# A two-layer hybrid trunk on one core: SSD groups with GLA heads between, and the decay logits on four row tiles

## The chip, the core and the metric

The kernel runs on one core of a Trainium2 chip. The metric is device time in microseconds. The kernel before takes 2295.11 us, the median of 3 runs (2294.96 to 2295.38).

## The reference, cut to what matters

Two layers (DEPTH = 2), a sequence of 512, D_MODEL = 1024, float32. Each layer projects the normed input to many parts at once and runs three branches on them:

```python
proj = u @ w_in
(gq, gk, gv, ga, gg, mqk, mv, mi, mf, mo, sz, sxbc, sdt, gates) = jnp.split(proj, SPLIT_POINTS, axis=-1)

log_a = jax.nn.log_sigmoid((ga @ gla_wa + gla_ba).astype(f32)) / GLA_TAU     # ga: 16 columns, gla_wa: 16 x 512
o_gla = gla(heads(gq, 4), heads(gk, 4), heads(gv, 4), heads(log_a, 4))
y_gla = group_rmsnorm(o_gla, gla_norm, GLA_HEADS) * silu(gg)
...                                                                          # mLSTM on mqk, mv, mi, mf, mo
xbc = silu(causal_dwconv(sxbc, ssd_conv_w, ssd_conv_b))
sx, sb, sc = split(xbc)                                                      # 16 heads of 64 in 2 groups
y = ssd(heads(sx, 16), softplus(sdt + bias), -exp(a_log), heads(sb, 2), heads(sc, 2))
y_s = group_rmsnorm((y + ssd_d * xh) * silu(sz), ssd_norm, SSD_GROUPS)

z = einsum('btkw,kwd->btkd', stack([y_gla, y_m, y_s]), w_branch)
h = h + sum(sigmoid(gates + gate_b) * z) @ w_out
h = h + conv_ffn(rmsnorm(h, norm_ffn), ...)                                  # width-3 conv, gated
```

Two things concern the change: the decay logits `ga @ gla_wa`, a product over 16 columns alone, and the SSD branch, whose two groups don't depend on each other.

## The kernel before, in words

Activations lie transposed: 128 channels on the partitions, 512 tokens along the free axis. Each large product is made exact to float32 by two fp32r parts of each operand, a rounded one (made by ScalarE, `act`) and the rest (made by VectorE, `tt`): three matmuls, high-high, high-low and low-high, take the place of one (`prods`). A projection of 128 output columns over 1024 input channels is 8 x 3 = 24 matmuls of 128 x 128 weights and 512 tokens. This is called a unit here. `units` makes two units from one pair of weight tiles; `units_tok` makes gv and mv with tokens on the partitions, at the same number of matmuls for 128 columns.

Weights stream from memory in the order of the list `MIX`: `load` issues a load on the SP queue into one of three raw buffers, and `prep` (priority 300) splits it into a high and a low part, in one of two buffers each. `S` is the first tile of a layer, the "small projections": columns 0 to 15 are ga, 32 to 47 sdt, 64 to 67 mi, 96 to 99 mf, the others zero. In the first layer `start` loads and splits the first two tiles in halves, between the tiles of the first norm.

The Python text gives the program order. The framework then plans each engine's instructions by its own cost estimates, in program order unless something is given priority (evictions of accumulators have 300, like `prep`), and writes out one fixed order for each engine; on the chip each engine takes its instructions in that order and waits where it must. Chains that don't belong to the units run in the background: `Bg` holds generators, and `after_unit` ticks all of them once after each unit. `bg.drain` ticks until a condition holds, without units in between. PSUM has four banks for accumulators of units and four (`mps`) for the small work.

The order in a layer (`layer`): S and twelve sxbc units with their convolutions (four taps on VectorE), while `rows` and both `ssd_group` generators run in the background; then for each two GLA heads, four units of gq and gk and four of gv; then `bg.drain` until all eight SSD outputs `sy` are there; then the four `gla_head` generators start (`stagger`, a lag of two ticks), beside eight units of sz (gate of the SSD branch), which complete the SSD branch's norm (`fin_s`); then the SSD branch's gates and output projection (`branch(u, 2, ...)`), mLSTM, gg, and so on to the MLP.

`rows` takes the output of S, called `sm`, and makes all per-token rows from it. Its first step after the biases (L524 to L529) is the decay logits: for each of four heads one float32 matmul of `wa` (128 x 128, of which 16 rows are not zero) with `sm`, and two reads of the result by ScalarE. `wa` is loaded by one DMA at the start of the layer (L877). `ssd_group` (L778) makes one group's scores (B times C), transposes its four x tiles and weights them, forms the states of the chunks, and then, for each pair of heads, the mixes (L830: a row broadcast by DMA, scalings, an exponential, a product) and two sets of small float32 matmuls: eight with 64 output columns (`bc`, `xd`) and three with 128 (`cc`, `ss`).

Of the kernel before, what the change touches and what calls it, by code (L numbers as in the profile page):

```python
# [9 lines left out]
F32 = mybir.dt.float32  # L10
F32R = mybir.dt.float32r
I32 = mybir.dt.int32
AF = mybir.ActivationFunctionType
ALU = mybir.AluOpType
# [3 lines left out]
P = 128  # L18
L = 2
D = 1024  # L20
T = 512
# [32 lines left out]
MIX = ["S"]  # L54
for _g in range(2):
    MIX += [("sxbc", 1024 + 128 * _g), ("sxbc", 1280 + 128 * _g)]
    MIX += [("sxbc", 512 * _g + 128 * _i) for _i in range(4)]
NSSD = len(MIX)

TOK = []  # L60
for _h in range(0, 4, 2):
    MIX += [("gq", 128 * _h), ("gk", 128 * _h), ("gq", 128 * _h + 128), ("gk", 128 * _h + 128)]
    TOK.append(len(MIX))
    MIX += [("gv", 256 * _h + 128 * _i) for _i in range(4)]
# [27 lines left out]
N8 = NMIX + 2 * NFF  # L92
# [41 lines left out]
class Kern:  # L134
# [122 lines left out]
    def load(self):  # L257
# [14 lines left out]
        self.raw_q.append(raw)  # L272
        self.load_at = [c, j + 1] if j + 1 < n else [c + 1, 0]

    def start(self):

        nc = self.nc
        nc.sync.dma_start(self.pars[0], self.par_in[0])
        half = KT // 2
        raws = []  # L280
        for j in range(2):
            self.n += 1
            raws.append(self.pw.tile([P, KT * P], F32, tag="raw", name=f"raw_{self.n}", bufs=RAW_BUFS))
        self.n += 1
        wh, wl = (self.pw.tile([P, KT, 2 * P], F32R, tag=t, name=f"{t}_{self.n}", bufs=W_BUFS) for t in ("wh", "wl"))
        self.split[0] = (wh, wl)
        for i in range(KT):
            self.h[i] = self.t("h")
        for k in range(2):
            ks = slice(k * half, (k + 1) * half)  # L290
            cs = slice(k * half * P, (k + 1) * half * P)
            nc.sync.dma_start(self.h[k * half], self.xT[:, k * half, :])
            for j in range(2):
                nc.sync.dma_start(raws[j][:, cs], self.w8[j][:, cs])
            for i in range(k * half + 1, (k + 1) * half):
                nc.sync.dma_start(self.h[i], self.xT[:, i, :])
        nc.sync.dma_start(self.cst, self.cst_in)
        for k in range(2):
            ks = slice(k * half, (k + 1) * half)
            cs = slice(k * half * P, (k + 1) * half * P)  # L300
            for j in range(2):
                r = raws[j][:, cs].rearrange("p (k c) -> p k c", c=P)
                o = slice(j * P, (j + 1) * P)
                self.act(wh[:, ks, o], r)
                self.tt(wl[:, ks, o], r, wh[:, ks, o].bitcast(F32), ALU.subtract)
            for i in range(k * half, (k + 1) * half):
                self.norm_tile(i)
                self.h[i] = None
        self.load_at, self.prep_at = [1, 0], [1, 0]
        self.load()  # L310
        nc.sync.dma_start(self.pars[1], self.par_in[1])
        for _ in range(RAW_BUFS - 1):
            self.load()
# [6 lines left out]
    def prep_(self):  # L320
        c, j = self.prep_at
        if c >= len(self.chunks):
            return
        if not self.raw_q:
            self.load()
        src, idx, nk, n = self.chunks[c]
        if src == 2:
            nk, n = KT // 2, 4
        raw = self.raw_q.pop(0)
        if j == 0:  # L330
            self.n += 1
            self.split[c] = (
                self.pw.tile([P, nk, n * P], F32R, tag="wh", name=f"wh_{self.n}", bufs=W_BUFS),
                self.pw.tile([P, nk, n * P], F32R, tag="wl", name=f"wl_{self.n}", bufs=W_BUFS))
        wh, wl = self.split[c]
        if src == 2:
            n = 2
            cs = slice(2 * j * P, 2 * (j + 1) * P)
            wh, wl = (w[:, :, cs].rearrange("p k (j c) -> p j k c", j=2) for w in (wh, wl))
            r = raw.rearrange("p j (k c) -> p j k c", c=P)  # L340
        else:
            wh, wl = wh[:, :, j * P:(j + 1) * P], wl[:, :, j * P:(j + 1) * P]
            r = raw.rearrange("p (k c) -> p k c", c=P)
        self.act(wh, r)
        self.tt(wl, r, wh.bitcast(F32), ALU.subtract)
        self.load()
        self.prep_at = [c, j + 1] if j + 1 < n else [c + 1, 0]
# [158 lines left out]
    def rows(self, ps):  # L506
# [12 lines left out]
        self.n += 1  # L519
        ag, ab = [la[:, h] for h in range(4)], la[:, 4]  # L520
        self.act(ab, zs, AF.Abs)
        zg = []
        yield
        for h in range(4):  # L524
            p2 = self.mps()
            self.mm(p2, self.wa[:, h * P:(h + 1) * P], sm)
            z = self.t("zg")
            self.act(z, p2, AF.Identity, bias=self.col("ba", h))
            self.act(ag[h], p2, AF.Abs, bias=self.col("ba", h))  # L529
            zg.append(z)  # L530
            if h == 1:
                yield
# [339 lines left out]
    def layer(self, l):  # L872
        nc = self.nc
        bg = self.bg
        self.par = self.pars[l]
        self.wa = self.pc.tile([P, T], F32, name=f"wa{l}", tag="wa", bufs=1)
        self.dq.dma_start(self.wa, self.wa_in[l])  # L877
        self.hpar = self.pc.tile([P, HHI - HLO], F32, name=f"hpar{l}", tag="hpar", bufs=2)
        nc.vector.tensor_scalar(self.hpar, self.par[:, HLO:HHI], 0.5, None, op0=ALU.mult)
        self.rows_ready = False  # L880
# [10 lines left out]
        def evx(i, store, j):  # L891
            def ev(ps):
                store[j] = self.silu2(*self.conv(ps, 4, "scw", i, 12, "scb", i))
            return ev
        evs = [lambda ps: bg.add(self.rows(ps))]
        for g in range(2):
            evs += [evx(8 + g, self.sb, g), evx(10 + g, self.sc, g)]
            evs += [evx(4 * g + i, self.sx, 4 * g + i) for i in range(4)]
        bg.add(self.ssd_group(0))
        bg.add(self.ssd_group(1))  # L900
        for i in range(0, NSSD, 2):
            self.wide = i < WIDE
            self.units(u, evs[i:i + 2], boundary=(i == 0), mid=(self.norm_end, self.norm_rows_of_cols))


        for h in range(4):
            def evq(ps):
                self.gq[h] = self.t("gq")
                with self.tc.high_priority(EV_PRIO):
                    self.stt(self.gq[h], ps, 128.0 ** -0.5, self.rstd, ALU.mult, ALU.mult)  # L910

            def evk(ps):
                self.gk[h] = self.t("gk")
                self.first(self.gk[h], ps)
            self.units(u, [evq, evk])
            if h % 2:
                for i in (h - 1, h):
                    self.gv[i] = Blocks([self.v() for _ in range(2)])
                self.units_tok(u, lambda b, ps: self.evac_tok(b, ps, self.gv[h - 1:h + 1]))
        bg.drain(lambda: full(self.sy))  # L920


        rsum_g = self.t("rsg")
        bg.add(self.stagger([self.gla_head(h, rsum_g) for h in range(4)], GLA_LAG))
        sqs, ready, ys, done_s = [None, None], [], [], []

        def fin_s(g):
# [21 lines left out]
        bg.add(fin_s(0))  # L949
        bg.add(fin_s(1))  # L950
        for g in range(2):
            for i in range(2):
                def evz(ps, j):
                    s = self.t("sz")
# [293 lines left out]
GLA_LAG = 2  # L1248
# [101 lines left out]
```

## Time and profile before

| | |
|---|---|
| median of 3 runs | 2295.11 us (2294.96 to 2295.38) |
| the profiled execution's own time | 2295.16 us |
| its span, first to last instruction | 2293.3 us |
| TensorE busy | 2279.3 us, 99% |
| VectorE busy | 1434.1 us, 63% |
| ScalarE busy | 902.7 us, 39% |
| mean granted TensorE clock | 0.998 of 2.4 GHz |
| DMA | 235.73 MB, 103 GB/s on average |

Busy means that an instruction of the engine was under way. Matmuls are pipelined, so a matmul's own duration (0.39 us for 512 columns) overlaps the next one's; the step from one start to the next is its price. A float32 matmul shows as two records. The rows below give times from the start of the span. In a row of the timeline the first number is the start, the second the duration, then engine, line, operation, output and inputs by the program's names, the shape, and the count of merged instructions; in brackets stands the engine's idle time before it and what ended it. L241 is the helper of every matmul, L229 that of every ScalarE instruction, L232 and L238 those of VectorE.

### The profile page before, as it was taken

The page shows a single profiled execution, that of the slowest core. Times are in us where ns is not written, and L with a number is a line of the kernel's source. Part 1 is how long each engine was busy: PE and PEld are TensorE (multiplying, and loading weights), DVE is VectorE, ACT ScalarE, POOL GpSimd, SP SyncE. Part 2 cuts the span into 40 slices and gives each one's busy share as a digit, 9 for nine tenths or more (in the row PEclk, how much of TensorE's full clock was granted, in tenths as well). Part 3 has the DMA queues.
Part 4 walks back from the last instruction along what each step waited for, and adds up shares of the span by engine and source line. Part 5 has one row for each costly group of instructions (what it writes and reads, how often), then busy time and mean ns, then how long its engine had stood idle before and what let it go on. Part 6 is the DMA issues. An engine that isn't in the chain of part 4 may idle for free.

```text
span 2293.3 us, 27258 instructions
## 1 busy us (share of the span) xinstructions
PE 2279.3 (99%) x10832; PEld 1876.8 (82%) x10832; DVE 1434.1 (63%) x2165; ACT 902.7 (39%) x1344; POOL 2.8 (0%) x22
## 2 busy tenths in 40 slices
PE   9999999999999999999999999999999999999998
PEld 6878888888888888888888788888888888888887
DVE  6966745474464587467579767345744645873774
ACT  6534632333333344234354346233333433442432
POOL 0000000000000000000000000000000000000000
PEclk9999999999999999999999999999999999999999
DMA  5253223332232333232323522232322343232222
GB/s 181 85 156 101 74 74 104 99 120 93 87 111 97 129 100 107 82 101 97 128 85 102 162 92 74 77 107 93 129 90 90 101 132 107 93 97 94 94 91 75
DMA packets 78911, 235.73 MB, mean 103 GB/s; under 512 B 8872, under 2 KB 12264, under 8 KB 78784
## 3 DMA queue, kind: packets, MB, share of 16 engines
q1 hardware_dynamic: 78784, 233.99, 31.7%
q8 instruction: 85, 1.39, 0.3%
q14 instruction: 42, 0.34, 0.1%
HBM read 229.55 MB, written 4.41 MB: 102 GB/s over the span
## 4 chain that ended last, share of the span: by engine, by line
PE 93%; DVE 4%; ACT 2%; issue 1%; DMA 1%; SPq 0%; DVEq 0%; ACTq 0%
PE acc L241 65%; PE m L241 27%; DVE cc L238 1%; PE m L244 1%; ACT la L229 1%; DVE wl L232 1%; DVE la L610 0%; DMA h<-in_xT 0%; DVE og L232 0%; DVE cx L232 0%; DMA dn<-ry 0%; ACT zg L229 0%; ACT cc L229 0%; DVE zg L238 0%; ACT wh L229 0%
## 5 line engine op out<-in xcount | busy, mean ns | idle before, releaser
L229 ACT ACTIVATE wh<-raw 128x1024 fp32r<-128x1024 f32 (+2 forms) x372 | 385.1, 1077 | 586.1 <-PE acc L241 250.9
L241 PE MATMUL acc<-uh,wh 128*128 128x512 f32 x1552 | 609.3, 393 | 2.0 <-DVE mo L232 1.0
L241 PE MATMUL acc<-uh,wl 128*128 128x512 f32 x1552 | 605.9, 391 | 0.4 <-DVE wl L232 0.3
L241 PE MATMUL acc<-ul,wh 128*128 128x512 f32 x1552 | 605.7, 390 | 0.1
L232 DVE TENSOR_TENSOR wl<-raw,wh 128x1024 fp32r<-128x1024 f32 (+2 forms) x372 | 453.2, 1250 | 154.4 <-ACT wh L229 154.0
L241 PEld LDWEIGHTS acc<-uh,wh 128*128 128x128 f32 x1552 | 291.4, 188 | 64.2 <-issue 2.7
L241 PEld LDWEIGHTS acc<-uh,wl 128*128 128x128 f32 x1552 | 291.4, 188 | 62.7 <-DVE wl L232 1.5
L241 PEld LDWEIGHTS acc<-ul,wh 128*128 128x128 f32 x1552 | 291.4, 188 | 61.6 <-DVE ul L238 1.6
L238 DVE SCALAR_TENSOR_TENSOR cc<-cx,par,cc 128x510 f32<-128x510 f32 (+2 forms) x296 | 217.6, 748 | 41.0 <-ACT cc L229 36.9
L241 PE MATMUL acc<-yl,wh 128*128 128x512 f32 x512 | 200.0, 391 | 0.0
L241 PE MATMUL acc<-yh,wl 128*128 128x512 f32 x512 | 199.7, 390 | 0.0
L241 PE MATMUL acc<-yh,wh 128*128 128x512 f32 x512 | 199.6, 392 | 0.0
L241 PE MATMUL m<-uh,wh 128*128 128x512 f32 x384 | 149.8, 390 | 1.2 <-ACT wh L229 1.2
L241 PE MATMUL m<-uh,wl 128*128 128x512 f32 x384 | 149.9, 390 | 0.0
L241 PE MATMUL m<-ul,wh 128*128 128x512 f32 x384 | 149.4, 389 | 0.0
L229 ACT ACTIVATE cc<-cx,par 128x512 f32<-128x512 f32 x128 | 102.8, 809 | 86.6 <-DVE cx L232 86.5
L241 PE MATMUL m<-ah,wl 128*128 128x512 f32 x308 | 120.0, 390 | 0.0
L241 PE MATMUL m<-al,wh 128*128 128x512 f32 x308 | 119.8, 389 | 0.0
L241 PE MATMUL m<-ah,wh 128*128 128x512 f32 x308 | 119.5, 389 | 0.0
L241 PEld LDWEIGHTS acc<-yh,wl 128*128 128x128 f32 x512 | 96.1, 188 | 20.5 <-issue 0.4
L241 PEld LDWEIGHTS acc<-yh,wh 128*128 128x128 f32 x512 | 96.1, 188 | 19.8 <-DVE gg L232 0.4
L241 PEld LDWEIGHTS acc<-yl,wh 128*128 128x128 f32 x512 | 96.2, 188 | 19.5
(204 smaller groups left out, 2653.3 us busy)
## 6 DMA issues: line engine op xcount, KB each, us to landing
raw<-in_w SPq DMA_DIRECT2D x336, 512.0 KB, 3.6
raw<-in_w SPq DMA_DIRECT2D x32, 704.0 KB, 4.0
bc<-dr SPq DMA_DIRECT2D x48, 256.0 KB, 3.6
h<-in_xT SPq DMA_DIRECT2D x16, 256.0 KB, 6.6
eb<-dr SPq DMA_DIRECT2D x32, 128.0 KB, 4.5
bc<-dn SPq DMA_DIRECT2D x16, 256.0 KB, 3.1
kept<-h SPq DMA_DIRECT2D x8, 256.0 KB, 2.0
h<-kept SPq DMA_DIRECT2D x8, 256.0 KB, 5.6
```

The source lines that it names most:

```text
L229: return self.nc.scalar.activation(out, in_, func, bias=bias, scale=scale)
L232: return self.nc.vector.tensor_tensor(out, a, b, op=op)
L238: return self.nc.vector.scalar_tensor_tensor(out, a, s, b, op0=op0, op1=op1)
L241: return self.nc.tensor.matmul(out, lhsT, rhs, start=start, stop=stop)
L244: return self.nc.tensor.transpose(out, x, self.ident)
```

## The change

It has two parts.

The order: `MIX` now has group 0 of the SSD projections (sb, sc and four sx tiles), two GLA heads' projections, group 1 of the SSD projections, and the other two GLA heads'. `layer` follows it with `ssd_proj(g)`. The first drain asks only for the four outputs of group 0; the second asks for the others ahead of the sz units of group 1, and the `gla_head` generators are added there instead of ahead of all sz units.

The decay logits: `spread` copies the columns of ga in the raw S tile to columns 48, 80 and 112, so that `sm` has ga in rows 0 to 15, 48 to 63, 80 to 95 and 112 to 127. The weights of head h are put in the same rows of one 128 x 128 tile, by eight loads, and split into a high and a low part, as is `sm`. Each head's logits are then three fp32r matmuls on 32 rows (rows 32h to 32h+31), in three passes over the heads, to four PSUM banks.

```diff
@@ MIX
 for _g in range(2):
     MIX += [("sxbc", 1024 + 128 * _g), ("sxbc", 1280 + 128 * _g)]
     MIX += [("sxbc", 512 * _g + 128 * _i) for _i in range(4)]
-NSSD = len(MIX)
-
-TOK = []
-for _h in range(0, 4, 2):
+    if _g == 0:
+        NSSD = len(MIX)
+
+        TOK = []
+    _h = 2 * _g
     MIX += [("gq", 128 * _h), ("gk", 128 * _h), ("gq", 128 * _h + 128), ("gk", 128 * _h + 128)]
     TOK.append(len(MIX))
     MIX += [("gv", 256 * _h + 128 * _i) for _i in range(4)]
@@ new
+    def spread(self, r):
+
+        o = r[:, :, 32:].rearrange("p k (g c) -> p k g c", c=32)[:, :, :, 16:]
+        self.nc.vector.tensor_copy(o, r[:, :, 0:16].unsqueeze(2).to_broadcast([P, r.shape[1], 3, 16]))
@@ start, for each half of the first two tiles
                 r = raws[j][:, cs].rearrange("p (k c) -> p k c", c=P)
+                if j == 0:
+                    self.spread(r)
@@ prep_
+        if src == 0 and idx % N8 == 0 and j == 0:
+            self.spread(r)
         self.act(wh, r)
@@ rows
+        sh, sl = self.split_tile(sm, "sx")
         zg = []
         yield
+        ps = [self.mps() for _ in range(4)]
+        wh, wl = self.wa
+        for w, x in ((wh, sh), (wh, sl), (wl, sh)):
+            for h in range(4):
+                r = slice(32 * h, 32 * h + 32)
+                self.mm(ps[h], w[r], x[r], start=(w is wh and x is sh), stop=(w is wl))
         for h in range(4):
-            p2 = self.mps()
-            self.mm(p2, self.wa[:, h * P:(h + 1) * P], sm)
             z = self.t("zg")
-            self.act(z, p2, AF.Identity, bias=self.col("ba", h))
-            self.act(ag[h], p2, AF.Abs, bias=self.col("ba", h))
+            self.act(z, ps[h], AF.Identity, bias=self.col("ba", h))
+            self.act(ag[h], ps[h], AF.Abs, bias=self.col("ba", h))
@@ layer
-        self.wa = self.pc.tile([P, T], F32, name=f"wa{l}", tag="wa", bufs=1)
-        self.dq.dma_start(self.wa, self.wa_in[l])
+        wa = self.small([P, P], "wa", 1)
+        for h in range(4):
+            hs = slice(h * P, (h + 1) * P)
+            r = 32 * h + (16 if h else 0)
+            self.dq.dma_start(wa[r:r + 16], self.wa_in[l][0:16, hs])
+            r = 32 * h + (0 if h else 16)
+            self.dq.dma_start(wa[r:r + 16], self.wa_in[l][16:32, hs])
+        self.wa = [self.ps.tile([P, P], F32R, tag=n, name=f"{n}{l}", bufs=1) for n in ("wah", "wal")]
+        self.act(self.wa[0], wa)
+        self.tt(self.wa[1], wa, self.wa[0].bitcast(F32), ALU.subtract)
@@ layer, the SSD projections
-        evs = [lambda ps: bg.add(self.rows(ps))]
-        for g in range(2):
+        bg.add(self.ssd_group(0))
+        bg.add(self.ssd_group(1))
+
+        def ssd_proj(g):
+            evs = [] if g else [lambda ps: bg.add(self.rows(ps))]
             evs += [evx(8 + g, self.sb, g), evx(10 + g, self.sc, g)]
             evs += [evx(4 * g + i, self.sx, 4 * g + i) for i in range(4)]
-        bg.add(self.ssd_group(0))
-        bg.add(self.ssd_group(1))
-        for i in range(0, NSSD, 2):
-            self.wide = i < WIDE
-            self.units(u, evs[i:i + 2], boundary=(i == 0), mid=(self.norm_end, self.norm_rows_of_cols))
+            for i in range(0, len(evs), 2):
+                self.wide = g == 0 and i < WIDE
+                first = g == 0 and i == 0
+                self.units(u, evs[i:i + 2], boundary=first, mid=(self.norm_end, self.norm_rows_of_cols))
@@ layer, ahead of each GLA head's projections
+            if h % 2 == 0:
+                ssd_proj(h // 2)
@@ layer, behind the GLA projections
-        bg.drain(lambda: full(self.sy))
+        bg.drain(lambda: full(self.sy[:4]))
-        bg.add(self.stagger([self.gla_head(h, rsum_g) for h in range(4)], GLA_LAG))
@@ layer, the sz units
         for g in range(2):
+            if g == 1:
+                bg.drain(lambda: full(self.sy[4:]))
+                bg.add(self.stagger([self.gla_head(h, rsum_g) for h in range(4)], GLA_LAG))
```

## Rows read from the trace of the kernel before

**Rows 1.** The page, busy time of each engine, share and instructions.
```profile
PE 2279.3 (99%) x10832; PEld 1876.8 (82%) x10832; DVE 1434.1 (63%) x2165; ACT 902.7 (39%) x1344; POOL 2.8 (0%) x22
```
**Rows 2.** The chain of waits: start us, length us, what.
```profile
655.45 130.85 PE acc L241 x576
```
**Rows 3.** Table by stretch: length, busy PE, PEld, DVE, ACT, POOL, clock, DMA.
```profile
0.00:31.00 31.00, 27.76 (x103) 18.63 (x104) 19.20 (x40) 17.36 (x27) 1.19 (x6) 1.00 0.75 258
...
57.00:115.00 58.00, 57.48 (x282) 47.81 (x281) 57.72 (x109) 30.61 (x50) 0.00 (x0) 1.00 0.29 84
115.00:147.00 32.00, 32.00 (x134) 24.46 (x133) 23.35 (x57) 12.73 (x21) 0.00 (x0) 1.00 0.39 123
147.00:200.00 53.00, 53.00 (x329) 41.36 (x328) 39.07 (x94) 14.70 (x22) 0.00 (x0) 1.00 0.47 144
```
**Rows 4.** Timeline of TensorE, the decay logits of the first layer.
```profile
37.88 3.60 PE L241 MATMUL m<-sm,wa 128*128 128x512 f32 x8
...
41.55 0.39 PE L241 MATMUL acc<-ul,wh 128*128 128x512 f32 x1
```
**Rows 5.** Timeline of TensorE, column sums of one column and of 32.
```profile
278.32 0.95 PE L241 MATMUL m<-cst,sq 128*128 128x1 f32 x8
279.19 0.43 PE L241 MATMUL m<-sqo,cst 128*32 128x128 f32 x8
279.55 0.71 PE L241 MATMUL m<-sct,v 128*128 128x128 f32 x4
```
**Rows 6.** Timeline of TensorE, two SSD head pairs.
```profile
166.71 1.09 PE L241 MATMUL m<-bc,xd 128*64 128x128 f32 x16
167.73 0.94 PE L241 MATMUL m<-cc,ss 128*128 128x128 f32 x6
168.42 0.47 PE L241 MATMUL acc<-uh,wl 128*128 128x512 f32 x1
...
187.68 0.43 PE L241 MATMUL m<-bc,xd 128*64 128x128 f32 x2
188.04 0.94 PE L241 MATMUL m<-cc,ss 128*128 128x128 f32 x6
188.73 0.48 PE L241 MATMUL acc<-wh,uh 128*128 128x512 f32 x1
189.14 1.09 PE L241 MATMUL m<-bc,xd 128*64 128x128 f32 x14
190.16 0.50 PE L241 MATMUL acc<-wh,ul 128*128 128x512 f32 x1
```
**Rows 7.** Groups of VectorE instructions, 0 to 330 us: count, busy, mean ns, idle before.
```profile
L837 DVE TENSOR_SCALAR bc<-bc,ca 128x128 f32<-128x128 f32 x64 | 13.9, 283 | 5.8 <-DMA bc<-dr 5.8
...
L232 DVE TENSOR_TENSOR yl<-y,yh 128x512 fp32r<-128x512 f32 x8 | 5.4, 686 | 0.0
```
**Rows 8.** Timeline of TensorE, the start.
```profile
8.17 0.51 PE L241 MATMUL m<-uh,wh 128*128 128x512 f32 x1 [1.22 <-ACT wh L229]
```
**Rows 9.** Timeline of ScalarE, the start.
```profile
7.49 0.63 ACT L229 ACTIVATE wh<-raw 128x512 fp32r<-128x512 f32 x1 [1.32 <-DMA raw<-in_w]
```
**Rows 10.** Timeline of the SP queue, loads behind the start.
```profile
10.62 0.33 SPq L311 DMA_DIRECT2D par<-in_par  x1
11.30 0.33 SPq L877 DMA_DIRECT2D wa<-in_wa  x1
15.72 0.93 SPq L271 DMA_DIRECT2D raw<-in_w  x2
```
**Rows 11.** Timeline of VectorE, last output of SSD group 1, first layer.
```profile
196.06 0.56 DVE L232 TENSOR_TENSOR y<-y,eb 128x384 f32<-128x384 f32 x1
```
**Rows 12.** Timeline of TensorE, first matmul of the SSD output projection.
```profile
289.78 0.47 PE L241 MATMUL acc<-yh,wh 128*128 128x512 f32 x1
```
**Rows 13.** Timeline of TensorE, last matmuls of the GLA heads, first layer.
```profile
313.47 0.43 PE L241 MATMUL m<-sqo,cst 128*32 128x128 f32 x8
```
**Rows 14.** Timeline of ScalarE, first reuse of the v buffers, for mLSTM.
```profile
398.48 0.84 ACT L229 ACTIVATE v<-acc,rcol 128x256 f32<-128x256 f32 x2 [0.94 <-PE acc L241]
```

## The prediction

> **What bounds the kernel now.** I read the busy line of the page first. TensorE is busy 2279.3 of 2293.3 us [rows 1]: 14.0 us of idle time in all, so an edit can gain only by taking TensorE work away, by closing some of those 14.0 us, or by making TensorE's work denser. Next, the chain of waits: its long pieces are matmuls alone, and one of them gives the price of an ordinary one, 130.85 us for 576, or 0.227 us each [rows 2]; a unit of 24 is 5.45 us. Then the table by stretch, over the start and the stage that the change reorders: in the latter TensorE loses 0.52 us in the 58 us where VectorE is busy for 57.72 us, and nothing in the two stretches after it [rows 3]. So the stage is bound by TensorE in spite of a full VectorE, and its order is worth little unless a new order breaks that. Last, the timeline of TensorE, for what small groups cost.
>
> **The change, part by part.**
>
> *Four float32 matmuls for the logits go.* They start at 37.88 us, and the second ordinary matmul after them starts at 41.55 us [rows 4]. Of these 3.67 us one ordinary matmul takes 0.23, so the four cost 3.44 us in each layer, 0.86 us each, on the path. Both layers: 6.9 us.
>
> *Twelve matmuls on 32 rows each come.* No row here has a tile of few rows. Upper bound: one after the other at the price of any matmul of 512 columns, 12 x 0.227 = 2.73 us. Lower bound: the four row tiles run fully side by side, 3 x 0.227 = 0.68 us. Two nearer rows: eight matmuls on 32 columns take 0.36 us (279.19 to 279.55) where eight full ones take 0.92 us by the six in 0.69 us [rows 5, 6], 2.5 times less, and 2.73 / 2.5 = 1.1 us. And eight matmuls of one column each take 0.87 us [rows 5], so a load of weights of 128 columns has a floor near 0.109 us; twelve such loads in a line are 1.3 us. I take 1.3, the dearer of the two near rows, since each row tile still loads 128 columns. Gain 3.44 - 1.3 = 2.1 us in a layer, **4.3 us** in both, with ends of 1.4 and 5.5.
>
> The short run is what can spoil this: a run of two narrow matmuls takes 0.36 us, where two of a run of sixteen take 2 x 0.064 = 0.13 [rows 6], so each short run pays 0.23 us. The Trainium skill has a rule on each side. "TensorE: Matmul & The Clock Gate", section "Measured speedup vs the span model", gives 3.07 times for four row tiles of 512 columns; by it the twelve are 0.89 us and the gain would be 5.1 us. "TensorEngine Tiling (Array Packing)", section "Key Properties", says a change of tiling mode drains the engine; the short runs agree with that, and if the planner cuts the twelve into their three passes with ordinary matmuls between, three times 0.23 brings the gain down to 2.9 us. No run here shows either for row tiles.
>
> *What these twelve wait for.* The first four need the rounded copy of `sm` on ScalarE, the other eight also the subtraction on VectorE: 0.69 us by a subtraction of the same shape [rows 7], and about as much on ScalarE. Behind them on TensorE stand the units' matmuls, in a fixed order; if the planner places the eight too early, TensorE idles for up to these 1.4 us. I take 0, since a unit's matmuls are there to fill the time; 2.8 us over both layers is the other end. The twelve hold all four small PSUM banks at once until ScalarE has read them; the small work that comes behind them in program order (transposes of the same rows) needs the logits' chain anyway.
>
> *The copies of columns (`spread`).* In the first layer two copies of 192 elements a partition stand on VectorE between a load's landing and ScalarE's rounding: by the row of 128 elements 0.28 us, by that of 512 0.69 [rows 7]; say 0.35 each. The first delays ScalarE's first rounding, but TensorE then sits idle for 1.22 us before 8.17 for the second tile's rounding, which waits for its own load [rows 8, 9], so it costs nothing. The second comes into the first norm, in the one stretch where TensorE has idle time to speak of, 3.24 of 31 us [rows 3]: +0.3 us, ends 0 and 0.7. In the second layer the copy is made a unit ahead: 0.
>
> *Decay weights.* Eight small loads instead of one: SP issues at 0.67 us spacing (10.62 to 11.30), so 5.4 us instead of 0.7; the next weight load, at 15.72 [rows 10], is pushed back by about 1 us. Behind it wait the next weight loads only, whose units lie two and more ahead; cost 0, and 1 us if that lead were gone. The rounding and subtraction of a 128 x 128 tile are about 0.3 us each on engines off the path: 0.
>
> *The order.* The amount of work stays. Group 1's six projections and convolutions go behind eight GLA units (8 x 5.45 = 44 us). Now the last output of group 1 is ready at 196.6 us and the first matmul that needs its normed form starts at 289.78 [rows 11, 12]. Moved by 44 us it is ready near 240, 50 us before: 0. If that cover were gone, TensorE would stand at 289.78 for the rest. GLA heads start four units (22 us) later; their last matmul is at 313.47, and their v buffers are first wanted again at 398.48 [rows 13, 14], so 63 us stay: 0.
> VectorE's crowded stretch loses six convolutions, so its 0.52 us of TensorE's time may go; I count -0.3 over both layers, ends -1 and +1, because group 0's mixes now meet group 1's convolutions.
> Density: a pair of heads' matmuls in one run takes 1.71 us (166.71 to 168.42); cut into two, with one ordinary matmul between, 2.48 - 0.23 = 2.25 (187.68 to 190.16) [rows 6], 0.54 us more. In the trace six of the eight pairs of the first layer are cut so and four of the second. The planner draws these anew; none cut would be 10 x 0.54 = -5.4 us, all sixteen cut 6 x 0.54 = +3.2. I take 0, with no reason for a side.
>
> **Sum.** -4.3 + 0.3 - 0.3 = -4.3 us. The profiled execution took 2295.16 us, 0.05 from the median of 2295.11, so the forecast is **2290.9 us**, 0.18% less. About 0.2% (4.6 us) is what a measurement of this kernel can tell from no change; the forecast lies just inside.
>
> **The rivals.**
> 1. *Row tiles don't overlap.* Twelve at 0.227: the gain is 1.4 us, and the time 2295.2 - 1.4 = 2293.8. For it: column tiles are all that the trace shows to overlap. Against it: 128x64 and 128x32 tiles both do [rows 5, 6].
> 2. *The new order makes TensorE's small work denser.* Five of the ten cuts fall away, 2.7 us: 2288.2. For it: less small work of two groups is live at once, so fewer heads compete. Against it: the mixes come later beside a busy VectorE, which is what cuts them.
> 3. *Slower: VectorE becomes the bound where group 1's convolutions meet group 0's mixes.* Now mixes lie in 147:200, where VectorE has 39.07 of 53 us, and convolutions in 57:115, full [rows 3]. One step of mixes is eight scalings at 0.28 us, two products at 0.69 and three passes of output (about 1.9): 5.5 us. It decides from the point where a unit's eviction, which releases one of four accumulators (four units, 22 us of lead), stands behind mixes that much of the lead has already gone to. One step so exposed in each layer: 2 x 5.5 = 11 us, 2290.9 + 11 = 2302. Against it: in the full 57:115 stretch TensorE lost 0.52 us alone, since evictions and weight preparation are put ahead, and 115:147 and 147:200 have 22 us of VectorE to spare.
>
> **How the numbers follow.** Forecast 0.60, rival 1 0.12, rival 2 0.13, rival 3 0.15. The forecast's own range, from the bounds of the row tiles (1.4 to 5.5) and a few cuts either way, is 2288 to 2293.5. With rivals 1 and 2 inside, and up to a small form of rival 3, the range is 2287.0 to 2296.0; most of rival 3 and some very dense orders stay out. Faster by over 0.2% means under 2290.5: somewhat under half of the forecast (0.27) and rival 2 (0.13), 0.40. Slower is rival 3, 0.15. Within 0.2% is the rest, 0.45.
>
> **What would show it.** Row tiles: matmuls of 32 rows with the twelve starting within about 1.3 us a layer; 2.7 us speaks for rival 1. Startup: TensorE's idle time before its second tile, now 1.22 us, shorter by the first copy. Order: VectorE under 58 us in 57:115, TensorE idle time not above 14 us; over 20 speaks for rival 3, with accumulating matmuls waiting for VectorE evictions. Density: the number of cut pairs, now ten. Wrong altogether would be a stretch past the GLA heads that differs in length between the two traces.

## The result, and the profile after

The changed kernel takes 2317.53 us (median of four runs, 2316.43 to 2319.33); the kernel before, beside it, 2295.24. The ratio is 1.0096, 95% interval 1.0079 to 1.0114: slower by 22 us, where the forecast was 2290.9. The profiled execution has a span of 2314.6 us, 21.3 more than before. The page's busy line:

```profile
PE 2283.1 (99%) x10840; PEld 1877.9 (81%) x10840; DVE 1437.2 (62%) x2172; ACT 906.9 (39%) x1348; POOL 2.8 (0%) x22
```

TensorE is idle for 2314.6 - 2283.1 = 31.5 us, against 14.0 [rows 1]. So 17.5 of the 21.3 us are idle time, and 3.8 us are busy time, although there is less work. What TensorE waited for (total us, times, longest; in the kernel after each helper's line is one higher, so L242 is every matmul and L245 a transpose):

```profile
PE m L245 <- DVE ra L233: 7.7, 2, 6.8
PE m L245 <- DVE cc L239: 6.7, 5, 2.8
PE acc L242 <- DVE cx L233: 2.1, 2, 1.1
```

In the kernel before, TensorE waits for none of the three longer than 0.52 us in all. `ra` is a row of the gates, `cc` a convolved x tile; both are transposed by TensorE. The table by stretch (length, busy PE, PEld, DVE, ACT, POOL, clock, DMA) for the stage in which they lie, to be read beside [rows 3]:

```profile
57.00:90.00 33.00, 25.97 (x109) 20.91 (x108) 29.22 (x43) 20.84 (x34) 0.00 (x0) 0.90 0.30 88
90.00:118.00 28.00, 28.00 (x140) 23.39 (x140) 13.97 (x38) 9.80 (x16) 0.00 (x0) 1.00 0.26 87
118.00:155.00 37.00, 37.00 (x167) 29.81 (x166) 23.70 (x43) 11.64 (x15) 0.00 (x0) 1.00 0.42 127
155.00:182.00 27.00, 21.22 (x113) 15.58 (x112) 25.20 (x63) 10.54 (x14) 0.00 (x0) 0.94 0.31 96
```

From 57 to 118 us VectorE has become less full, not fuller: 43.2 of the 61 us. In the last stretch, where group 1's x tiles are made, it is nearly full: 25.2 of 27. TensorE loses 7.0 us in the first stretch and 5.8 in the last, and in both its clock falls.

**The row tiles** did nearly what was forecast of them. The timeline of TensorE, first layer (start us, duration, what):

```profile
39.68 0.50 PE L242 MATMUL m<-sxh,wah 32*128 32x512 f32 x3
40.11 0.50 PE L242 MATMUL acc<-uh,wl 128*128 128x512 f32 x1
40.54 0.50 PE L242 MATMUL m<-sxl,wah 32*128 32x512 f32 x2
...
40.88 0.62 PE L242 MATMUL m<-sxh,wal 32*128 32x512 f32 x3
41.44 0.50 PE L242 MATMUL acc<-uh,wh 128*128 128x512 f32 x1
41.78 0.40 PE L242 MATMUL acc<-ul,wh 128*128 128x512 f32 x1
```

The four float32 ones were priced up to the second ordinary matmul behind them, 3.44 us [rows 4]. Measured in the same way, from the first of the twelve to the second ordinary matmul behind them, it is 2.10 us with two ordinary ones inside, so the twelve cost 1.65 us. In the second layer it is 1.64 (1185.35 to 1187.44, with two inside). The gain is 3.6 us in both layers together.

**The first loss: the rows' transposes.** Up to 72 us TensorE is ahead of the kernel before. Then:

```profile
72.66 0.39 PE L242 MATMUL acc<-uh,wl 128*128 128x512 f32 x1
79.87 1.12 PE L245 MATMUL m<-cst,ra 128*128 128x128 f32 x4 [6.82 <-DVE ra L233]
81.20 0.79 PE L242 MATMUL acc<-wh,uh 128*128 128x512 f32 x1 [0.21 <-DVE gq L239]
81.79 0.63 PE L242 MATMUL acc<-wh,ul 128*128 128x512 f32 x1
```

In the kernel before, the same four transposes, the chain on VectorE that makes their operand, and the exponential and logarithm on ScalarE (the two `la<-la` lines) stand so (timelines of the three engines):

```profile
74.69 0.60 PE L244 MATMUL m<-cst,ra 128*128 128x128 f32 x4
```
```profile
59.99 3.45 DVE L610 TENSOR_TENSOR_SCAN la<-cst,zg 128x512 f32<-128x512 f32 x3
...
68.92 1.22 DVE L551 TENSOR_TENSOR_SCAN bt<-cst,u 128x512 f32<-128x512 f32 x1
...
73.74 0.69 DVE L232 TENSOR_TENSOR ra<-ig,bt 32x512 f32<-32x512 f32 x1
```
```profile
38.95 0.69 ACT L229 ACTIVATE zg<-m,par 128x512 f32<-128x512 f32 x1 [1.92 <-PE m L241]
...
45.45 2.39 ACT L229 ACTIVATE la<-la 128x2560 f32<-128x2560 f32 x1
...
52.07 2.35 ACT L229 ACTIVATE la<-la 128x2560 f32<-128x2560 f32 x1
```

`ra` was ready at 74.43 and wanted at 74.69: 0.26 us of slack. After, TensorE is there at 72.66 + 0.23 = 72.89, 1.80 us sooner, and `ra` is ready at 79.13 + 0.69 = 79.82, 5.39 later: 1.80 + 5.39 - 0.26 = 6.9, and the trace has 6.82. So the stop eats the row tiles' gain in that layer as well. Where the 5.4 us come from, on ScalarE and VectorE after:

```profile
41.52 0.67 ACT L230 ACTIVATE zg<-m,par 128x512 f32<-128x512 f32 x1
...
47.49 2.04 ACT L230 ACTIVATE wh<-raw 128x1024 fp32r<-128x1024 f32 x2
49.39 2.38 ACT L230 ACTIVATE la<-la 128x2560 f32<-128x2560 f32 x1
...
55.03 1.06 ACT L230 ACTIVATE wh<-raw 128x1024 fp32r<-128x1024 f32 x1 [1.28 <-DMA raw<-in_w]
...
57.41 2.35 ACT L230 ACTIVATE la<-la 128x2560 f32<-128x2560 f32 x1
```
```profile
60.40 2.49 DVE L239 SCALAR_TENSOR_TENSOR zg<-zg,la 128x512 f32<-128x512 f32 x4
...
65.39 4.56 DVE L626 TENSOR_TENSOR_SCAN la<-cst,zg 128x512 f32<-128x512 f32 x4
...
74.11 1.22 DVE L567 TENSOR_TENSOR_SCAN bt<-cst,u 128x512 f32<-128x512 f32 x1
...
79.13 0.69 DVE L233 TENSOR_TENSOR ra<-ig,bt 32x512 f32<-32x512 f32 x1
```

The float32 matmuls gave head after head, and ScalarE read the first at 38.95. The three passes give all four heads at the end, and they start 1.8 us later, behind the rounding and the subtraction: the first read is at 41.52, 2.6 later. A pair of weight roundings (1.9 us) now comes ahead of the exponential, which is 3.9 later; two more stand between it and the logarithm, one of them after a wait of 1.28 us for its load, and the logarithm is 5.3 later. So the delay is complete by the logarithm, 2.6 us of it from the logits and the rest from the order on ScalarE. VectorE only passes it on: its rows' scan (`bt`) is 5.2 later, at 74.11 for 68.92. Ahead of that scan stand four GLA subtractions and four GLA scans (7.0 us), whose results are wanted by nothing on TensorE until the GLA heads. They stand there in the kernel before as well (55.06 to 65.2), so they are no part of the 5.4 us, but they are time that the chain could be given back.

**The second loss: the transposes of group 1's x tiles.** In the kernel before TensorE never waits for them; the last ones start 4.4 us after their convolution is finished (TensorE, then VectorE, before):

```profile
125.08 0.60 PE L244 MATMUL m<-cst,cc 128*128 128x128 f32 x4
```
```profile
119.95 0.69 DVE L238 SCALAR_TENSOR_TENSOR cc<-cx,cc 128x512 f32<-128x512 f32 x1
```

Now, on TensorE:

```profile
158.45 1.11 PE L245 MATMUL m<-cst,cc 128*128 128x128 f32 x4 [2.75 <-DVE cc L239]
159.50 1.98 PE L242 MATMUL m<-bc,xd 128*64 128x128 f32 x16
...
176.79 0.63 PE L245 MATMUL m<-cst,cc 128*128 128x128 f32 x4 [0.85 <-DVE cc L239]
```

`cc` is finished at 158.40. VectorE was late with it because it stood 3.06 us before a scaling of group 0's mixes, for a row that SP issued only behind three weight loads. These took it 11.51 us, where two took 0.93 in [rows 10]; by the program such a load waits for one of three raw buffers, and SP's waits in the trace name the subtraction that frees one (`wl` on VectorE). SP stands so in the kernel before too, up to 15.9 us at once in its first 200 us, but there no x tile hangs on the rows that come late. VectorE, then SP's queue:

```profile
154.88 0.87 DVE L853 TENSOR_SCALAR bc<-bc,ca 128x128 f32<-128x128 f32 x4 [3.06 <-DMA bc<-dr]
155.66 0.74 DVE L239 SCALAR_TENSOR_TENSOR cc<-cx,par,cc 128x509 f32<-128x509 f32 x1
```
```profile
136.49 11.51 SPq L268 DMA_DIRECT2D raw<-in_w  x3
148.10 0.89 SPq L512 DMA_DIRECT2D bc<-dr  x2
```

The second layer has the same two places (1224.30: 0.87 and 0.67 us; 1300 to 1312: 0.86, 1.74 and 1.07).

### The profile page after: what moved, and what is told of

It is laid out like the page before. It is cut to its first block, busy times and chain, and to the rows that moved or that the text cites. A ratio compares the mean times of both kernels' runs of the same rounds, so it can differ in the third digit from the quotient of the medians.

```text
span 2314.6 us, 27321 instructions
## 1 busy us (share of the span) xinstructions
PE 2283.1 (99%) x10840; PEld 1877.9 (81%) x10840; DVE 1437.2 (62%) x2172; ACT 906.9 (39%) x1348; POOL 2.8 (0%) x22
## 4 chain that ended last, share of the span: by engine, by line
PE 90%; DVE 5%; DMA 2%; ACT 1%; issue 1%; SPq 0%; DVEq 0%; ACTq 0%
PE acc L242 63%; PE m L242 27%; DVE wl L233 1%; DVE cc L239 1%; PE m L245 1%; ACT la L230 1%; DMA bc<-dr 1%; DVE og L233 0%; DVE la L626 0%; DMA raw<-in_w 0%; DMA dn<-ry 0%; DMA bc<-dn 0%; DMA h<-in_xT 0%; ACT wh L230 0%; DVE nt L239 0%
## 5 line engine op out<-in xcount | busy, mean ns | idle before, releaser
L242 PE MATMUL acc<-uh,wh 128*128 128x512 f32 x1536 | 603.6, 393 | 3.8 <-DVE cx L233 2.1
L242 PE MATMUL acc<-uh,wl 128*128 128x512 f32 x1536 | 600.1, 391 | 0.0
L242 PE MATMUL acc<-ul,wh 128*128 128x512 f32 x1536 | 599.5, 390 | 0.0
L242 PEld LDWEIGHTS acc<-uh,wh 128*128 128x128 f32 x1536 | 288.9, 188 | 66.2 <-issue 6.3
L242 PEld LDWEIGHTS acc<-uh,wl 128*128 128x128 f32 x1536 | 288.8, 188 | 60.9 <-issue 1.3
L242 PEld LDWEIGHTS acc<-ul,wh 128*128 128x128 f32 x1536 | 288.8, 188 | 59.6 <-issue 0.5
L239 DVE SCALAR_TENSOR_TENSOR cc<-cx,par,cc 128x511 f32<-128x511 f32 (+2 forms) x296 | 218.5, 747 | 45.5 <-ACT cc L230 41.4
L242 PE MATMUL acc<-yl,wh 128*128 128x512 f32 x512 | 200.4, 391 | 0.0
L242 PE MATMUL acc<-yh,wh 128*128 128x512 f32 x512 | 199.9, 393 | 0.0
L242 PE MATMUL acc<-yh,wl 128*128 128x512 f32 x512 | 199.7, 390 | 0.0
L242 PE MATMUL m<-uh,wh 128*128 128x512 f32 x400 | 156.0, 391 | 1.5 <-ACT wh L230 1.5
L242 PE MATMUL m<-uh,wl 128*128 128x512 f32 x400 | 156.3, 391 | 0.1
L242 PE MATMUL m<-ul,wh 128*128 128x512 f32 x400 | 156.0, 390 | 0.1
L242 PE MATMUL m<-ah,wl 128*128 128x512 f32 x308 | 120.1, 390 | 0.0
L242 PE MATMUL m<-al,wh 128*128 128x512 f32 x308 | 119.8, 389 | 0.0
L242 PE MATMUL m<-ah,wh 128*128 128x512 f32 x308 | 119.5, 389 | 0.0
L242 PEld LDWEIGHTS acc<-yh,wl 128*128 128x128 f32 x512 | 96.1, 188 | 20.2 <-issue 0.4
L242 PEld LDWEIGHTS acc<-yl,wh 128*128 128x128 f32 x512 | 96.2, 188 | 19.7 <-issue 0.4
L242 PEld LDWEIGHTS acc<-yh,wh 128*128 128x128 f32 x512 | 96.0, 188 | 19.7 <-DVE gg L233 0.4
```

Of the source, the lines that this page charges most:

```text
L239: return self.nc.vector.scalar_tensor_tensor(out, a, s, b, op0=op0, op1=op1)
L242: return self.nc.tensor.matmul(out, lhsT, rhs, start=start, stop=stop)
```

## The experiments

The kernel before took 2295.97 to 2296.3 us beside all of them.

**The two parts alone.** `e1` is the new order with the float32 logits, `e2` the row tiles (with `spread` and the split weights) in the old order; each is the change with the other part's lines put back.

> The changed order alone: the logits are again four float32 matmuls, with one load of their weights and no copies of columns. In the changed kernel TensorE idles in two places, waiting for VectorE: 6.8 us in front of the transposes of the rows (ra) in the first layer and 0.9 us in the second, and about 4 us and 2.6 us in front of the transposes of group 1's x tiles, with matmuls at half clock behind several of these. Theory A, the row tiles' longer chain (copy, subtraction, twelve matmuls before the first read) makes the rows late and the order makes the x tiles late: here the wait for ra is near the 0.5 us of before and the wait for the x tiles stays; the time is 2317.5 - 8 to 10 (ra, with its slow matmuls) + 4 (float32 matmuls back) = about 2312. Theory B, the order alone makes both: the ra wait stays too, about 2321. Theory C, the row tiles make both: about 2295.

> The row tiles alone, with the order of before. Theory A (the tiles' chain makes the rows late): TensorE waits for ra by several us in the first layer, 2295.2 - 4 + 8 to 10 = about 2300. Theory B (the order makes both waits): no such wait, and only the gain of the row tiles is seen, 2295.2 - 3.9 = about 2291.3, within 2290 to 2293. Theory C (tiles make all of it): about 2317.

`e1`: 2312.45 us, ratio 1.0075 (1.006 to 1.009). `e2`: 2302.64, 1.0029 (1.0017 to 1.0041). Against the 2296.3 us beside them these are +16.2 and +6.3, together +22.5, about the +22 of the whole change. In `e1` the wait for `ra` is gone and the waits for x tiles stay; in `e2` one wait stands at the place of the rows, for an eviction that VectorE has behind the rows' late products, and the clock falls after it (waits of `e1`; timeline and stretches of `e2`):

```profile
PE m L245 <- DVE cc L239: 6.4, 5, 1.8
```
```profile
79.11 0.77 PE L241 MATMUL acc<-uh,wh 128*128 128x512 f32 x1 [6.06 <-DVE cx L232]
```
```profile
79.10:83.40 4.30, 4.29 (x10) 0.50 0.21 85
84.00:90.00 6.00, 6.00 (x30) 1.00 0.03 5
```

Theory A holds: each part costs by itself, at its own place.

**Is it the mixes?** `e3` lets group 0's mixes wait until group 1's last x tile is convolved.

```diff
+        while g == 0 and self.sx[7] is None:
+            yield
```

> The changed kernel, but group 0's mixes may not begin until the last convolution of group 1 has been traced, so that the mixes no longer stand between group 1's convolutions on VectorE. Theory D, the x tiles are late since mixes are in the way on VectorE (by their load, or by their rows, which land late): the 4 + 2.6 us in front of the x transposes and the half-clock matmuls behind them go, about 9 us, so 2307 to 2310. Theory E, the transposes simply come one unit behind their convolutions, without slack, whatever else VectorE does: the waits stay, 2315 to 2319. The 6.8 us for ra stay under both.

2360.3 us, 1.028 (1.0265 to 1.0296): far outside what either theory allowed. The longest waits of TensorE:

```profile
PE acc L242 <- DVE sz L233: 22.6, 6, 5.8
```

Pushed back, the mixes meet the evictions of the sz units, and those hold up TensorE for 22.6 us. That is rival 3's mechanism, in a place where the change itself doesn't have it. The waits for x tiles fall from 6.7 to 2.9 us, but with TensorE held up elsewhere as much as this, that decides nothing about them.

**Is it the slack of the transposes?** `e4` holds the x transposes of a group until all its four convolutions are in; `e14` does the same to the new order alone. This is more than the kernel before has: there seven of the eight x tiles are transposed by 113.9 us, ahead of the last convolution's end at 120.64.

```diff
@@ ssd_group, ahead of the x tiles
+        while self.sx[4 * g + 3] is None:
+            yield
```

> The changed kernel, but a group's x transposes begin only when its last convolution has been traced, so that each comes three units behind its convolution instead of one. Theory E (no slack between a convolution and its transposes): the waits for the x tiles go, about 9 us, 2307 to 2310. Theory D (mixes in the way on VectorE): three units are 16 us, more than the longest wait of 2.8 us, so most of the wait goes too, but VectorE stays behind and TensorE waits elsewhere for it (evictions cx, or the first matmuls of the states), 2311 to 2316. The 6.8 us for ra stay under both.

> The new order alone, with the float32 logits of before, and the x transposes held until all four convolutions of their group are in. Theory A+E (the two causes are separate and add: the tiles' late chain costs at the rows' products, the order at the x transposes): the x waits go, about 12.5 us less than the order alone, 2300 us or a little below, and no wait for ra. Rival K (the two causes share a stall, so that taking the transposes' waits away from the order alone gives back less than it gave in the full change): 2304 to 2309, with waits elsewhere, gq or the evictions.

`e4`: 2305.04 us, 1.0041 (1.0027 to 1.0055), 12.5 us less than the change and 2 us below what theory E allowed. No wait for `cc` is left; of the long ones this stays, and in the stretch where TensorE lost 5.8 us it now loses nothing beside a VectorE that is as full as in the change, 25.2 us (TensorE's waits; table by stretch):

```profile
PE m L245 <- DVE ra L233: 7.6, 2, 6.7
```
```profile
155.00:182.00 27.00, 27.00 (x148) 21.22 (x147) 25.19 (x69) 7.58 (x10) 0.00 (x0) 1.00 0.43 128
```

So it is the slack and not the load of VectorE.

`e14`: 2300.06, 1.0018 (1.0009 to 1.0028), 12.4 less than `e1`, as theory A+E has it. The two causes are separate. `e14` stays 4 us above the kernel before, and little of that is waiting: in its trace TensorE's idle time is 1.4 us longer and its busy time 3.9 us.

**Is it the lateness of the rows' chain?** `e5` is `e4` with the GLA subtractions and scans ordered behind the rows' products on VectorE; `e6` does it to `e2`, and `e7` to the kernel before.

```diff
-        self.tt(r1[q], bt[q], m[q], ALU.subtract)
+        last = self.tt(r1[q], bt[q], m[q], ALU.subtract)
...
-            self.stt(zg[h], zg[h], 0.0, ag[h], ALU.min, ALU.subtract)
-            nc.vector.tensor_tensor_scan(bb, self.scanmask, zg[h], ...)
+            with self.tc.issue_after(last.ins):
+                self.stt(zg[h], zg[h], 0.0, ag[h], ALU.min, ALU.subtract)
+                nc.vector.tensor_tensor_scan(bb, self.scanmask, zg[h], ...)
```

> The changed kernel with x transposes three units behind their convolutions (as in the run before) and, in rows, the four GLA subtractions and four GLA scans ordered on VectorE behind r1, the second of the two subtractions that the rows need. Theory F, TensorE's 6.7 us wait for ra comes from these eight GLA instructions (about 7 us) that stand ahead of the rows' own scan on VectorE though nothing needs them for another 150 us: the wait goes with the half-clock matmuls behind it, 2305.0 - 8 to 10 = 2295 to 2297. Theory G, the rows' chain is late from its start (logits read 2.6 us later, the first exponential 3.9 us later): VectorE idles in place of the eight, most of the wait stays, 2301 to 2305.

> The row tiles alone, in the order of before, with the same eight GLA instructions behind r1 on VectorE. Theory F: the wait of 6.1 us for an eviction at 72.7 us goes, with the slow matmuls behind it: 2302.6 - 7 to 8 = 2295, less what a denser TensorE gives; with the tiles' gain seen in full 2291. Theory G: 2299 to 2303.

> The kernel before with the eight GLA instructions behind r1 on VectorE, nothing else. Both theories: no wait of that size is there to remove (0.52 us in the first layer, 0.3 in the second), so 2294.5 to 2296; a change of more than 2 us would say that the planner's new drawing of the order moves TensorE's time by itself.

`e5`: 2296.58 us, 1.0004 (0.9995 to 1.0013): the wait for `ra` is gone, 8.5 us less than `e4`, and the whole loss is made good, as theory F has it. The chain is still late at its start, as theory G says; the 7 us given back on VectorE outweigh that. `e7`: 2296.05, 0.9999 (0.999 to 1.0009), no change, so the edit is worth something only where the chain is late. `e6`: 2303.16, 1.0028 (1.0017 to 1.0039), no better than `e2`. That is near theory G's time, but not by its mechanism: the wait at 72.7 is gone, as theory F has it, but another came (TensorE, then VectorE's waits from 100 to 200 us):

```profile
179.97 0.77 PE L241 MATMUL acc<-wh,uh 128*128 128x512 f32 x1 [5.09 <-DVE gq L238]
```
```profile
DVE bc L852 <- DMA bc<-dr: 10.4, 7, 4.6
```

An eviction stands on VectorE behind mixes that wait for their rows. That led to a third suspect, the SP queue.

**The row tiles, or the lateness alone?** `e8` gives the split, the twelve matmuls and ScalarE's eight reads high priority (in the old order). `e9` has no row tiles: the kernel before, its float32 logits fed by a copy of `sm` that went twice through ScalarE and once through VectorE.

```diff
+        s0, s1, s2 = self.t("sa"), self.t("sc"), self.t("sd")
+        self.act(s0, sm)
+        self.act(s1, s0)
+        nc.vector.tensor_scalar(s2, s1, 0.0, None, op0=ALU.add)
...
-            self.mm(p2, self.wa[:, h * P:(h + 1) * P], sm)
+            self.mm(p2, self.wa[:, h * P:(h + 1) * P], s2)
```

> The row tiles alone, in the order of before, with the copy and subtraction of sm, the twelve matmuls and the eight reads of the logits given the same priority as evictions. Theory G: the logits are read up to 2.6 us sooner, the exponential follows, and the wait of 6.1 us shrinks by as much or more: 2297 to 2300. Theory F: the GLA scans still stand ahead of the rows' scan, the wait stays near 6 us, 2301 to 2304.

> The kernel before, with nothing of the change, but the logits' float32 matmuls read a copy of sm that went through two copies on ScalarE and one on VectorE, so that the rows' chain starts about 2 us later. Theory G' (lateness at the start of the rows' chain, from whatever cause, makes TensorE wait at 72 to 80 us): the first exponential comes at 47 us or later (45.45 before), TensorE waits several us there, 2297 to 2303. Rival H (it is something else of the row tiles, as their eight loads, the copied columns or the four banks held at once): the wait stays near 0.5 us, 2295.5 to 2297.

`e8`: 2302.24 us, 1.0027 (1.0016 to 1.0038). The first read came only 0.6 us sooner than in `e2` (41.89 for 42.47) and the pair of roundings stayed ahead of the exponential: it didn't do what it was to do, and tells nothing. `e9`: 2304.91, 1.0037 (1.0024 to 1.0051), 2 us above the range of theory G'. Its first read is at 43.45, 4.5 us later than in the kernel before, the roundings jump the exponential, and the same transposes wait (ScalarE; waits of TensorE):

```profile
49.43 2.04 ACT L229 ACTIVATE wh<-raw 128x1024 fp32r<-128x1024 f32 x2
51.33 2.38 ACT L229 ACTIVATE la<-la 128x2560 f32<-128x2560 f32 x1
```
```profile
PE m L244 <- DVE ra L232: 5.1, 1, 5.1
```

So lateness at the start of the chain is enough to make a loss of this kind, without any row tile; in the change it is the row tiles that make the chain late.

**The queue of the mixes' rows.** The loads of `bc` and `eb` go to GpSimd's queue instead of SP's: `e10` on `e6`, `e11` on the change, `e12` on the kernel before, `e13` on `e5`.

```diff
-                e = self.bcast(dr[16 + hd:17 + hd])
+                e = self.t("bc")
+                nc.gpsimd.dma_start(e, dr[16 + hd:17 + hd].partition_broadcast(P))
...
-            self.dq.dma_start(e2[0:64], ...)
+            nc.gpsimd.dma_start(e2[0:64], ...)
```

> The row tiles alone with the GLA instructions behind r1 (2303.2 us), and the loads of the mixes' rows (bc, eb) issued on GpSimd's queue instead of SP's. There VectorE waited 9.0 us in 140 to 182 us for the rows, which stand on SP behind weight loads that wait for a free buffer, and TensorE then waited 5.1 us for an eviction of gq behind them. Theory I (the SP queue makes the rows late): VectorE's wait and the 5.1 us go, with the slow matmuls behind: 2303 - 7 = 2296, or 2292 if the tiles' gain comes through. Rival J (GpSimd's queue is slower to land, or VectorE is merely full): the waits stay or grow, 2301 or more.

> The changed kernel with the mixes' rows loaded on GpSimd's queue. TensorE waits 2.75 us at 155 us for an x tile whose convolution stands on VectorE behind scalings that wait 3.1 us for their row. Theory I: this wait goes (with the slow matmuls behind it about 5 us), the other waits for x tiles without such a row ahead stay, so 2312 to 2314. Rival J: 2317 or more. Theory E alone (no slack between convolution and transposes): 2315 to 2318.

> The kernel before with the mixes' rows loaded on GpSimd's queue, nothing else; a control. TensorE waits nowhere there for such a row, so both theories: 2294 to 2297, unless GpSimd's loads land so late that VectorE falls behind (rival J: over 2298).

> The changed kernel with the x transposes held until all four convolutions of their group are in, the GLA scans behind the rows' products on VectorE (as in the version that took 2296.6 us), and the SSD mixes' row loads on GpSimd's queue instead of SP's. Theory I (loads behind SP's weight loads cost the mixes, and through VectorE TensorE, a few us wherever the mixes meet waiting evictions): no wait above 1 us for gq or wl in the first layer, and 2290 to 2294 us, below the kernel before. Rival J (with both waits gone the row loads cover nothing that TensorE needs, and the queue's change alone costs the 2 to 3 us that it cost the kernel before): 2296 to 2299.

`e10`: 2297.21 us, 1.0004 (0.9994 to 1.0013), 6.0 less than `e6`; the 5.09 us wait is gone and VectorE's wait for rows is a quarter (100 to 200 us):

```profile
DVE bc L853 <- DMA bc<-dr: 2.4, 3, 1.3
```

The Trainium skill says ("DMA: Bandwidth & Descriptors", section "Issuing engines are not separate DMA queues") that issuing from several engines saves only the sequencer's issue time, usually small beside the DMA itself. In this order it was worth 6 us: the time on the sequencer is not small where it stands at loads that can't start yet, as for the 11.51 us shown above.

`e11`: 2316.39, 1.0085 (1.0068 to 1.0102), 1 us less than the change, which the spread of the runs doesn't tell from nothing: the wait at 155 went and another for an x tile came, at 167 (waits of TensorE below). So the queue was what made the first tile late, but it is the missing slack, theory E, by which any lateness costs:

```profile
PE m L245 <- DVE cc L239: 4.6, 2, 2.3
```

`e12`: 2298.72, 1.0013 (1.0004 to 1.0022): 2.7 us more than the kernel before, above what theory I allowed, though TensorE's idle time is the same (14.2 us for 14.0). VectorE's wait for the rows from 100 to 200 us is no shorter there (7.3 us for 5.8), so the other queue isn't quicker by itself. `e13`: 2295.48, 1.0001 (0.9991 to 1.0011), between the two forecasts; 2.1 us of wait for a gq eviction remains. No version is measurably faster than the kernel before.

## Why the prediction was wrong

**Row tiles, 1.3 us for twelve: right in kind, a little low.** They cost 1.65 and 1.64; the gain was 3.6 us, not 4.3. Rival 1 (2.73 us) is out. The Trainium skill's 3.07 times ("TensorE: Matmul & The Clock Gate", section "Measured speedup vs the span model") gave an estimate of 0.89 us for them, which the trace doesn't reach. The Trainium skill's drain at a change of mode ("TensorEngine Tiling (Array Packing)", section "Key Properties"), charged as in the prediction with 0.23 us for each short run, makes that estimate 1.35 for the two runs that the trace shows, and 1.58 for the three that the prediction feared; both stay below the 1.65.

**"What these twelve wait for" taken as 0: the first step that failed.** It asked what the twelve wait for, and what fills TensorE meanwhile, and that was right: no stop lies there. It didn't ask who waits for what they give. It even named the transposes of the same rows and went on without a price. They had 0.26 us of slack in the trace of before; the rounding, the subtraction and the order in passes make the chain 2.6 us late at its first read, and the fixed order on ScalarE turns this into 5.3, which VectorE passes on. Price, by `e4` and `e5`: 8.5 us; by `e2`: 6.3 net of the tiles' gain.

**"The order", 0 with 50 and 63 us of cover: the second step that failed.** The covers held. The last output of group 1 and the first matmul that needs its normed form, after (VectorE, TensorE):

```profile
225.03 0.56 DVE L233 TENSOR_TENSOR y<-y,eb 128x384 f32<-128x384 f32 x1
```
```profile
288.08 0.58 PE L242 MATMUL acc<-yh,wh 128*128 128x512 f32 x1
```

That is 62 us [rows 11, 12]. The GLA heads end at 349.4 and their v buffers are wanted again at 412.24, 63 us later, as forecast, and the stretch from there to the MLP is as long as before (256.6 us, 257.0 before). But the slack at the end of a moved block says nothing about the waits inside it. When both groups came first, the generators couldn't start on their x tiles until the rows were ready (first scores at 91.5 us), when most of the convolutions were done, and even the last transposes had 4.4 us. With group 1 behind GLA units its rows are there already, so the generator follows each convolution at once, and TensorE's fixed order has the transposes right behind: three of the four x tiles in the first layer were waited for, and started 0.05 to 0.15 us after their convolution. Any delay on VectorE then stops all units. `e4` and `e14` put this at 12.5 us.

**VectorE's crowded stretch, -0.3: VectorE did empty there.** It has 43.2 of 61 us; the 0.3 us can't be told apart beside the 7.0 us that TensorE loses in the same stretch to the rows. Rival 3 had the side and one of the two places, with 0.15, but not the mechanism. Where group 1's convolutions meet group 0's mixes VectorE is nearly full, 25.2 of 27 us, but in `e4` it is as full there and TensorE loses nothing; and evictions of `cx`, its sign, cost 2.1 us in all. Its time of 2302 had 11 us for one cause; there were two, and 2317.5.

**Startup, +0.3: 0.** TensorE is busy for 27.80 us up to 31, against 27.76 [rows 3]. The sign was that the wait of 1.22 us gets shorter; it is one wait of 1.49 now, in place of that one and another of 0.47 ahead of it.

**Density, 0 with no side: a loss, by more than the pairs.** Eight pairs of heads are split into two and fourteen, against ten: by the prediction's 0.54 us, -1.1. (Three of those ten have no ordinary matmul in the gap, only their own other matmuls; the price is about the same, 2.27 us from 158.80 to 161.07.) But pairs are not all the small work that the new order splits. Call a matmul ordinary if it has 128 x 128 weights, 512 columns and fp32r parts, and small otherwise. Counted in the traces from 31 us on, TensorE goes over from ordinary to small matmuls 105 times in the kernel before, 117 times in the changed one, 128 in `e14` and 130 in `e5`. The ordinary matmuls beside small ones take, above 0.227 us each, 16.6 us before, 17.7 after, 19.4 in `e14` and 19.8 in `e5`. These 2.9 us are most of the 3.9 by which `e14` is busier than the kernel before, and 3.3 us of the same kind use up nearly all that the row tiles bring in `e5`. In `e12`, 2.0 us lie in the small matmuls themselves and 1.0 in the ordinary ones beside them. So rival 2's term had the other sign: the new order cuts TensorE's small work into more pieces, the more so with the transposes held. Whether the planner can draw it denser is not shown.

**The busy time.** It grew by 3.8 us where the tiles took 3.6 away, so 7.4 were added. By the steps of the trace, small matmuls take 4.2 of them, ordinary ones beside small ones 1.1, and ordinary ones elsewhere 2.1, these nearly all at a step of 0.43 us instead of 0.23. The small ones lie after stops in the main, as the sixteen at 159.50 (1.98 us, 1.09 in [rows 6]): in `e4`, without the waits for x tiles, 3.2 of the 4.2 are gone.

## What to carry to other kernels

When a step is replaced by a cheaper one on the busiest engine, price its latency too: find the instruction on that engine that consumes the chain's result, and read from the trace how long before it the result was ready. When a block of work is moved, read that slack at every place where the busiest engine takes a result from inside the block, not only at its end; an engine that takes its instructions in a fixed order waits for the first that isn't ready, with work behind it that is. Count how often the new order takes the busiest engine from its large pieces to its small ones, for each change has its price. Where a transfer is issued late, look at what its issuing queue stands at before asking how busy the DMA is.

## What the runs showed of the hardware

A stop can cost more than its length. After the 6.06 us in `e2` the granted clock was 0.50, the lower of the two levels (1.2 GHz), for 4.3 us: ten matmuls took 0.43 us each instead of 0.23, 2.0 us on top, a third of the stop. The same follows the stops at 72.9 and 155.7 us of the changed kernel, with a granted clock of 0.50 (79.9 to 83.0) and 0.53 (158.5 to 162.0). It didn't follow every stop: behind the 1.54 us in `e14` the next step was an ordinary one, with a clock of 1.00 in that stretch.
